# A hybrid encoder layer: narrower edge units in the attention, keys loaded once, the meta tokens' parts side by side, a factor product moved

## The chip, the core and the metric

The kernel runs on one core of a Trainium2 chip. Of the core's engines, TensorE (PE in the profile; its weight loads are listed apart as PEld) does all matrix products and transposes and writes them to PSUM, VectorE (DVE) and ScalarE (ACT) do the elementwise work and bring results out of PSUM, GpSimd (POOL) does small things here, and SyncE (SP) issues nearly all transfers. The metric is the time of one execution in microseconds (us), median of the runs; lower is better.

## The reference

The layer is applied to a prompt of 1024 tokens and a sample of 2048 tokens, each with the same 16 learned meta tokens in front. With `D = 1024`:

```python
xn   = rmsnorm(h, g_pre)
proj = xn @ w_in + b_in                      # 1024 -> 6672 columns
ya   = neighbourhood_attention(q, k, v, rpb) * silu(z)      # 8 heads of 64
yb   = mlstm(qk, v, gates, o) * silu(z)                     # 4 heads of 128, both directions
y    = (sigmoid(ga) * (ya @ w_a) + sigmoid(gb) * (yb @ w_b)) @ w_out
out  = h + rmsnorm(y, g_post)                # meta tokens dropped
```

In the attention the tokens form a grid of 64 columns. A query attends to the 16 meta tokens and to a window of 8 rows by 16 columns around it, with a relative bias. The reference takes query columns in four blocks of 16; each block looks at 32 key columns, which start at column 0, 8, 24 and 32 for the four blocks, and masks those outside a query's own window. For the leftmost block, windows reach from column 0 to 22 (the first 9 queries all have the window 0 to 15); for the rightmost they reach from 40 to 63. So of the 32 key columns of an edge block at most 24 can be in any window.

## The kernel before

All products keep near-float32 precision: each float32 operand is split into a high part (a copy to the type fp32r) and a low part (the difference), and a product is a sum of three: high by high, low by high, high by low. `mm3` (lines 169 to 171) issues such a triple with a weight part stationary and 512 tokens moving; `tm_unit` (lines 590 to 592) issues it with 128 tokens stationary and 256 or 264 weight columns moving.

Two streams are interleaved in program order on TensorE, which is fixed by the program; the other engines' orders come from a scheduler. `dense` yields the projections (`group`, `fm_half`, `tm_unit`) and, later, the output stage (`final`, lines 1569 to 1571 among others). `sparse` yields the mLSTM (`ml`) and the attention (`na`). Each `yield` hands over a cost in us, and `run` lets `dense` go on until it has used up what `sparse` yielded; when `sparse` has ended, the rest of `dense` runs alone. The steps are: mLSTM of the prompt, attention of the prompt, mLSTM of the sample, attention of the sample.

**The attention.** A *head* here is 8 query rows of one attention head (48 of them: 16 for the prompt, 32 for the sample). It takes 11, 12 or 15 key rows plus one row slot for the meta tokens, so 12, 13 or 16 slots. A *unit* is one of the head's four query blocks (192 units). A unit goes through a pipeline, four quarters per unit, `A_NA` = 1.085 yielded after each:

- `na_scores`: two products into one PSUM bank (`sc` or `sm`), with 128 queries stationary and all slots by 32 key columns moving (line 877 with the key's high part doubled in `kd`, line 878 with the low part and the mask rows in `kx`), so 384, 416 or 512 moving columns; then the bias and the row's extreme on VectorE (line 881).
- `na_exp` (ACT, line 891), one unit later `na_scale` (DVE, lines 899 and 900), one more later `na_turn`: four transposes (line 908) into bank `tr`, one for each 8 key columns, and the copy of the high part to `pts` (ACT, 910); `na_low` takes the low part (DVE, 915).
- `na_out`: four products with the values `vt` (line 923) into `sm`; `na_copy` and `na_add` bring the result out (lines 931, 938).

`na_prep` prepares the next head in steps during the units of the current one. The raw keys `kr` arrive in 64 partitions twice (`twice`, line 746: two transfers for the grid's keys, two for the meta tokens' keys), since the score product wants the high part in both halves of `kd`; ACT copies `kd` from `kr` in 128 partitions (line 855) and DVE makes the low part `kx` in 64 (line 857). The meta tokens' keys lie in the row slot at columns 8 to 23 and 32 to 47, so that each block of 32 key columns holds a whole copy, and the mask rows let one copy through.

**The meta tokens** go through `tm_unit` as 16 stationary columns: for each of 8 slices of D three products of 256 or 264 columns (five such units: 40 triples). The result is scaled by the token's factor `rc` and the bias is added in one DVE operation (line 601).

**The opening.** The first group (prompt tokens 0 to 511, then 512 to 1023) is projected before the norm's factors of its tokens are known. The four units of a half write to PSUM, and only when `rwait` has issued the factor product (`rrows`, line 320: ones times a diagonal, which spreads the factors over the partitions) may the results be scaled and leave. Up to then their banks are held: three of tag `pj`, which the next `tm_unit` needs too, and one of `tr`.

Of the kernel before, what the change touches and what calls it, by code (L numbers as in the profile page):

```python
# [42 lines left out]
KC0 = (0, 8, 24, 32)  # L43
OFFC = (15, 7, 7, -1)
# [27 lines left out]
def _consts():  # L72
# [9 lines left out]
    for typ, tl in ((0, 0), (1, 1), (2, R // 8 - 1)):  # L82
# [3 lines left out]
        for si, row in enumerate(slots):  # L86
            for c0 in range(49):
                m = np.full(64, NEG, np.float32)
                if row is None:
                    m[(8 if c0 < 24 else 32):][:NM] = 0.0  # L90
                else:
                    m[c0:c0 + 16] = 0.0
                masks[typ, c0, si] = m
# [27 lines left out]
class K:  # L121
# [231 lines left out]
    def opening(self, xp):  # L353
# [45 lines left out]
        self.wrp = wp, 2  # L399

# [93 lines left out]
    def fm_evac(self, col, s, t0, meta, chunks, ps):  # L494
# [39 lines left out]
        if meta and C_NK <= col < C_NV:  # L534
# [3 lines left out]
            nc.gpsimd.tensor_copy(km[:, 32:48], st[:, :NM])  # L538
# [31 lines left out]
    def tm_unit(self, col, halves, wd):  # L570
# [10 lines left out]
        for j, (x, s, c, n, cnt, tok) in enumerate(todo):  # L581
            st = wp.tile([P, 2, WU], F32, name="stT", bufs=4)
            for a in range(cnt):
                p = self.psum("pj", [P, 512])
                o = p[:n, :wd]
                xs = slice(c + a * P, c + a * P + n)
                for k in range(KT):
                    wh, wl = ws[k // 4][0][:, k % 4, :], ws[k // 4][1][:, k % 4, :]
                    xh, xl = x[0][:, k, xs], x[1][:, k, xs]
                    nc.tensor.matmul(o, xh, wh, start=k == 0, stop=False)  # L590
                    nc.tensor.matmul(o, xh, wl, start=False, stop=False)  # L591
                    nc.tensor.matmul(o, xl, wh, start=False, stop=k == KT - 1)  # L592
# [6 lines left out]
                if s == 0:  # L599
                    r = 8 if tok is None else tok // P + a  # L600
# [5 lines left out]
                yield 12 * C256  # L606

    def tm_store(self, col, wd, s, n, cnt, tok, st):
# [30 lines left out]
        else:  # L639
            if tok is None:  # L640
                for lo in (8, 32):
                    nc.sync.dma_start(self.NVM[lo:lo + NM, f:f + wd], st[:n, 0, :wd])
# [48 lines left out]
    def group(self, s, t0, meta, cols, reuse, nxt):  # L691
# [4 lines left out]
        for j, (kind, c) in enumerate(jobs):  # L696
# [7 lines left out]
            for hf in range(2):  # L704
# [37 lines left out]

    def twice(self, out, d, r0, c0):

        for a in (0, 64):
            self.nc.sync.dma_start(out[a:a + 64], d[r0:r0 + 64, c0:c0 + out.shape[1]])
# [70 lines left out]
    def na_prep(self, np_, s, rows, heads, j):  # L817
# [14 lines left out]
        self.twice(kr[:, rs:rs + nr, :].rearrange("p a b -> p (a b)"), self.NK[s][pr], h0, lo * 64)  # L832
        self.twice(kr[:, ms, :], self.NKM[pr], h0, 0)
# [20 lines left out]
        with self.held():  # L854
            nc.scalar.activation(kd[:, :ns, :], kr[:, :ns, :], AF.Copy)
        yield
        nc.vector.tensor_tensor(kx[0:64, :ns, :], kr[0:64, :ns, :], kd[0:64, :ns, :].bitcast(F32), op=ALU.subtract)
# [9 lines left out]
    def na_scores(self, np_, unit, rows):  # L867
# [8 lines left out]
        so = sc[:, :N].rearrange("p (a b) -> p a b", b=32)  # L876
        nc.tensor.matmul(so, stk[:, cb, :], kd[:, :ns, kc:kc + 32], start=True, stop=False)
        nc.tensor.matmul(so, qb[:, cb, :], self.kx[hh][:, :ns, kc:kc + 32], start=False, stop=True)
# [3 lines left out]
            out=so, in0=so, in1=gt[:, g0:g0 + ns, c0:c0 + 32],  # L882
            op0=ALU.add, op1=ALU.min, scale=-1.0, scalar=3.0e38, accum_out=mx)
        unit[3] = (pr_, mx, N)
        unit[6] = sc

    def na_exp(self, np_, unit):
        nc = self.nc
        (pr_, mx, N), sc = unit[3], unit[6]
        sm = np_.tile([P, 1], F32, name="sm", bufs=4)  # L890
        nc.scalar.activation(pr_[:, :N].rearrange("p (b a c) -> p b a c", b=4, c=8),
                             sc[:, :N].rearrange("p (a b c) -> p b a c", b=4, c=8),
                             AF.Exp, bias=mx, scale=-1.0, accum_out=sm)
        unit[3] = (pr_, sm, N)

    def na_scale(self, np_, unit):
        nc = self.nc
        pr_, sm, N = unit[3]
# [3 lines left out]
    def na_turn(self, np_, unit):  # L902
        nc = self.nc
        pr_, _, N = unit[3]
        ks = N // 4
        pt = self.psum("tr", [P, 4, P])
        for ch in range(4):
            nc.tensor.transpose(pt[:ks, ch, :], pr_[:, ch * ks:(ch + 1) * ks], self.ident)  # L908
        pts = np_.tile([P, 4, 2, P], F32R, name="pts", bufs=2)
        nc.scalar.activation(pts[:ks, :, 0, :], pt[:ks], AF.Copy)  # L910
        unit[4], unit[6] = pts, pt

    def na_low(self, unit):
        pts, pt, ks = unit[4], unit[6], unit[3][2] // 4
        self.nc.vector.tensor_tensor(pts[:ks, :, 1, :], pt[:ks], pts[:ks, :, 0, :].bitcast(F32), op=ALU.subtract)  # L915

    def na_out(self, unit):
        nc = self.nc
        vt, cb, (_, _, N), pts = unit[0][3], unit[2], unit[3], unit[4]
        ks, kc = N // 4, KC0[cb]  # L920
# [858 lines left out]
```

## Time and profile before

| | |
|---|---|
| median of 3 runs | 2786.84 us (2786.1 to 2787.6) |
| profiled execution | 2792.15 us, its span 2790.4 us |
| PE busy | 2764.9 us (99%), 17120 matmuls |
| PEld, DVE, ACT busy | 2461.8 us, 1828.0 us, 1311.8 us |
| attention of the prompt: first to last score product | 758.6 to 1111.1 us, 64 units |
| attention of the sample | 1926.8 to 2656.1 us, 128 units |

In the profile's views a row gives line, engine, operation, output and inputs by the program's names, and sizes. Matmuls overlap: one lasts from its start to the modelled end of its results, while the next has already begun. So what a matmul costs TensorE is read from start to start in the timeline, not from its duration. An "x4" in the timeline is four equal instructions in a row, with the time from the first start to the last end. A window view gives for each stretch its length, then the busy time and count of each engine, the granted clock and the DMA engines' share.

### The profile page before, as it was taken

Reading aid. Unit: us, or ns where it says so; the run is one execution under the profiler, and the core shown is the slowest. Engines: PE = TensorE matmul, PEld = TensorE weight load, DVE = VectorE, ACT = ScalarE, POOL = GpSimd, SP = SyncE. Lnnn points to the kernel's source line nnn. Section 1 sums busy time; section 2 is a strip of 40 time slices with the busy share of each in tenths; the row PEclk is TensorE's granted clock in tenths of the full one; section 3 lists DMA queues with packets and bytes.
Section 4 is the critical chain, followed back from the end, with each engine's and each line's share of the span. In section 5 each row is a group of like instructions: output and inputs, shape, how many; then the busy total and the mean of one; then the engine's idle time right before and its main releaser. Section 6 shows DMA issues by size and latency. Waiting matters only on the chain.

```text
span 2790.4 us, 48772 instructions
## 1 busy us (share of the span) xinstructions
PE 2764.9 (99%) x17120; PEld 2461.8 (88%) x17120; DVE 1828.0 (66%) x5075; ACT 1311.8 (47%) x3183; POOL 16.3 (1%) x103
## 2 busy tenths in 40 slices
PE   9999999999999999999999999999999999999998
PEld 7998898999899988988988888888888988889898
DVE  5232688676556655457767666584679888797954
ACT  5112556445443444255456555463455645445421
POOL 0000000000000000000000000000000000000000
PEclk9999999999999999999999999999999999999999
DMA  9555768755965544685666786666579898988965
GB/s 370 181 186 195 255 199 320 269 179 184 338 216 179 173 151 147 187 300 173 205 199 210 254 290 192 190 197 185 179 228 352 278 324 258 316 276 281 329 236 210
DMA packets 378277, 655.09 MB, mean 235 GB/s; under 512 B 50896, under 2 KB 199840, under 8 KB 378032
## 3 DMA queue, kind: packets, MB, share of 16 engines
q1 hardware_dynamic: 376912, 649.29, 70.5%
q0 software_dynamic: 1120, 2.69, 0.4%
q8 instruction: 135, 2.21, 0.3%
q14 instruction: 110, 0.90, 0.1%
HBM read 449.61 MB, written 202.22 MB: 234 GB/s over the span
## 4 chain that ended last, share of the span: by engine, by line
PE 92%; DMA 5%; DVE 2%; ACT 1%; issue 0%; SPq 0%; DVEq 0%; ACTq 0%
PE pj L169 16%; PE pj L170 16%; PE pj L171 16%; PE pj L590 7%; PE pj L591 7%; PE pj L592 7%; PE sm L923 3%; PE pj L1569 3%; PE pj L1571 3%; PE pj L1570 3%; PE tr L908 3%; DMA wraw<-wu 1%; DMA whi<-wh 1%; PE sm L171 1%; PE sm L170 1%; PE sm L169 1%
## 5 line engine op out<-in xcount | busy, mean ns | idle before, releaser
L169 PE MATMUL pj<-xh,whi 128*128 128x512 f32 (+1 forms) x1792 | 705.4, 394 | 1.5 <-ACT whi L263 1.3
L170 PE MATMUL pj<-xl,whi 128*128 128x512 f32 (+1 forms) x1792 | 689.7, 385 | 0.3 <-DVE xl L335 0.3
L171 PE MATMUL pj<-xh,wlo 128*128 128x512 f32 (+1 forms) x1792 | 688.2, 384 | 0.0
L590 PE MATMUL pj<-whi,xh 128*128 128x256 f32 (+3 forms) x1576 | 449.2, 285 | 1.5 <-ACT st L520 1.5
L591 PE MATMUL pj<-wlo,xh 128*128 128x256 f32 (+3 forms) x1576 | 443.7, 282 | 0.8 <-DMA wlo<-wl 0.8
L592 PE MATMUL pj<-whi,xl 128*128 128x256 f32 (+3 forms) x1576 | 443.6, 282 | 0.0
L171 PEld LDWEIGHTS pj<-xh,wlo 128*128 128x128 f32 x1792 | 337.2, 188 | 71.5 <-DVE wlo L264 0.2
L169 PEld LDWEIGHTS pj<-xh,whi 128*128 128x128 f32 x1792 | 337.3, 188 | 61.8 <-ACT whi L263 2.1
L170 PEld LDWEIGHTS pj<-xl,whi 128*128 128x128 f32 x1792 | 337.7, 188 | 57.5 <-issue 1.0
L590 PEld LDWEIGHTS pj<-whi,xh 128*128 128x128 f32 (+1 forms) x1576 | 293.5, 186 | 3.2 <-ACT st L520 1.9
L591 PEld LDWEIGHTS pj<-wlo,xh 128*128 128x128 f32 (+1 forms) x1576 | 293.1, 186 | 2.1 <-DMA wlo<-wl 1.1
L592 PEld LDWEIGHTS pj<-whi,xl 128*128 128x128 f32 (+1 forms) x1576 | 293.1, 186 | 0.9
L1569 PE MATMUL pj<-whi,mh 128*128 128x256 f32 x768 | 221.6, 289 | 3.6 <-DMA whi<-wh 3.6
L1570 PE MATMUL pj<-wlo,mh 128*128 128x256 f32 x768 | 217.6, 283 | 1.2 <-DMA wlo<-wl 1.2
L1571 PE MATMUL pj<-whi,mlo 128*128 128x256 f32 x768 | 217.7, 283 | 0.0
L915 DVE TENSOR_TENSOR pts<-tr,pts 96x512 fp32r<-96x512 f32 (+2 forms) x192 | 131.8, 686 | 96.0 <-ACT pts L910 95.1
L910 ACT ACTIVATE pts<-tr 96x512 fp32r<-96x512 f32 (+2 forms) x192 | 113.9, 593 | 136.8 <-PE tr L908 136.5
L169 PE MATMUL pj<-yh,whi 128*128 128x512 f32 x384 | 154.4, 402 | 0.0
L1569 PEld LDWEIGHTS pj<-whi,mh 128*128 128x128 f32 x768 | 146.4, 191 | 6.2 <-DMA whi<-wh 4.7
L171 PE MATMUL pj<-yh,wlo 128*128 128x512 f32 x384 | 151.4, 394 | 0.0
L170 PE MATMUL pj<-yl,whi 128*128 128x512 f32 x384 | 150.9, 393 | 0.0
L1570 PEld LDWEIGHTS pj<-wlo,mh 128*128 128x128 f32 x768 | 146.7, 191 | 3.0 <-DMA wlo<-wl 1.4
(283 smaller groups left out, 4990.4 us busy)
## 6 DMA issues: line engine op xcount, KB each, us to landing
whi<-wh SPq DMA_DIRECT2D x176, 512.0 KB
wlo<-wl SPq DMA_DIRECT2D x176, 512.0 KB
wraw<-wu SPq DMA_DIRECT2D x64, 512.0 KB
wh<-whi SPq DMA_DIRECT2D x64, 512.0 KB
wl<-wlo SPq DMA_DIRECT2D x64, 512.0 KB
gt<-st SPq DMA_DIRECT2D x96, 256.0 KB
tg<-gt SPq DMA_DIRECT2D x96, 256.0 KB
xt<-xt SPq DMA_DIRECT2D x32, 512.0 KB
```

Of the source, the lines that this page charges most:

```text
L169: mm(out, ah, bh, start=start, stop=False)
L170: mm(out, ah, bl, start=False, stop=False)
L171: mm(out, al, bh, start=False, stop=stop)
L590: nc.tensor.matmul(o, xh, wh, start=k == 0, stop=False)
L591: nc.tensor.matmul(o, xh, wl, start=False, stop=False)
L592: nc.tensor.matmul(o, xl, wh, start=False, stop=k == KT - 1)
L908: nc.tensor.transpose(pt[:ks, ch, :], pr_[:, ch * ks:(ch + 1) * ks], self.ident)
L910: nc.scalar.activation(pts[:ks, :, 0, :], pt[:ks], AF.Copy)
L915: self.nc.vector.tensor_tensor(pts[:ks, :, 1, :], pt[:ks], pts[:ks, :, 0, :].bitcast(F32), op=ALU.subtract)
L1569: nc.tensor.matmul(o, mh[:, k, xs], wh, start=k == 0, stop=False)
L1570: nc.tensor.matmul(o, mh[:, k, xs], wl, start=False, stop=False)
L1571: nc.tensor.matmul(o, ml[:, k, xs], wh, start=False, stop=k == KT - 1)
```

## The change

- **Edge units.** The first and the fourth block of a head take 24 key columns, from column 0 and 40 on (`NKB` holds the number of 8-column pieces, 3 or 4). Scores, bias, exponent and scale work on 24 columns per slot, with three transposes and three value products. The second copy of the meta tokens' keys moves to columns 40 to 55, the value rows and their zero rows accordingly.
- **Keys loaded once.** `kr` is loaded in one half (two transfers in place of four); ACT makes the high part in 64 partitions and copies it to the other 64 in a second operation.
- **Meta parts side by side.** A small tile `xmp` holds the meta tokens' high part in columns 0 to 15, zeros, and the low part in columns 32 to 47 of 48 stationary columns. Two products (by the weight's high and low part) replace three; the two partial results, in different partitions, are added by an ACT copy and a DVE addition ahead of the scaling. The new low-by-low term is part of the result for those partitions. `xmp` is filled in the opening and given back when the attention begins.
- **Factor product a unit sooner.** For the second half of the first group, `rwait` is called after the last step of unit 2 in place of the third step of unit 3, and the three units' results leave then; unit 3 alone goes to `tr`.

```diff
-KC0 = (0, 8, 24, 32)
-OFFC = (15, 7, 7, -1)
+KC0 = (0, 8, 24, 40)
+NKB = (3, 4, 4, 3)
+OFFC = (15, 7, 7, 7)
...
@@ opening
+        nc.gpsimd.memset(self.xmp[:, :, NM:2 * NM].bitcast(F32), 0.0)
+        for a in range(2):
+            nc.vector.tensor_copy(self.xmp[:, :, 2 * NM * a:2 * NM * a + NM], x[a][:, :, :NM].bitcast(F32))
...
@@ tm_unit
+                    if tok is None:
+                        both = self.xmp[:, k]
+                        nc.tensor.matmul(o, both, wh, start=k == 0, stop=False)
+                        nc.tensor.matmul(o, both, wl, start=False, stop=k == KT - 1)
...
-                        yield 12 * C256
+                        yield (8 if tok is None else 12) * C256
...
+                if tok is None:
+                    nc.scalar.activation(st[:n, 1, :wd], p[2 * NM:2 * NM + n, :wd], AF.Copy)
+                    nc.vector.tensor_tensor(st[:n, 1, :wd], p[:n, :wd], st[:n, 1, :wd], op=ALU.add)
+                    nc.vector.scalar_tensor_tensor(st[:n, 0, :wd], st[:n, 1, :wd], self.rc[:n, 8:9], bb[:n, :wd], op0=ALU.mult, op1=ALU.add)
...
@@ group
-                    lu = 3 if hf else 2
...
-                        if late is not None and u == lu and q == 2:
+                        if late is not None and u == 2 and q == 2 + hf:
                             self.rwait[todo[hf][:2]]()
-                    if late is not None and u == lu:
+                    if late is not None and u == 2:
                         for evac in late:
                             evac()
-                        late = tags = None
+                        late = None
+                        tags = iter(("tr",)) if hf else None
...
@@ na_prep
-        self.twice(kr[:, rs:rs + nr, :].rearrange("p a b -> p (a b)"), self.NK[s][pr], h0, lo * 64)
-        self.twice(kr[:, ms, :], self.NKM[pr], h0, 0)
+        nc.sync.dma_start(kr[0:64, rs:rs + nr, :].rearrange("p a b -> p (a b)"), self.NK[s][pr][h0:h0 + 64, lo * 64:(lo + nr) * 64])
+        nc.sync.dma_start(kr[0:64, ms, :], self.NKM[pr][h0:h0 + 64, :])
...
-            nc.scalar.activation(kd[:, :ns, :], kr[:, :ns, :], AF.Copy)
+            nc.scalar.activation(kd[0:64, :ns, :], kr[0:64, :ns, :], AF.Copy)
         yield
+        nc.scalar.activation(kd[64:128, :ns, :], kd[0:64, :ns, :].bitcast(F32), AF.Copy)
...
@@ na_scores
-        N, kc, g0 = ns * 32, KC0[cb], (5, 1, 0)[typ]
+        kc, nb, g0 = KC0[cb], NKB[cb], (5, 1, 0)[typ]
+        w, N = 8 * nb, 8 * nb * ns
...
@@ na_turn
-        for ch in range(4):
+        for ch in range(nb):
             nc.tensor.transpose(pt[:ks, ch, :], pr_[:, ch * ks:(ch + 1) * ks], self.ident)
...
@@ na_out
-        for ch in range(4):
+        for ch in range(nb):
             nc.tensor.matmul(av[:, :256], vt[:ks, kc // 8 + ch].rearrange("p a b -> p (a b)"),
```

Three places in the instruction orders show what moves. On TensorE in the opening, before, the factor product (`ones`, into `sm`) stands six matmuls ahead of the end of the second half's fourth unit (the one that writes `tr`); line 590 is the next `tm_unit`:

```order
L171 MATMUL tr<-xh,wlo 128x512
L320 MATMUL sm<-xr,ones 128x512
L169 MATMUL tr<-xh,whi 128x512
L170 MATMUL tr<-xl,whi 128x512
L171 MATMUL tr<-xh,wlo 128x512
L169 MATMUL tr<-xh,whi 128x512
L170 MATMUL tr<-xl,whi 128x512
L171 MATMUL tr<-xh,wlo 128x512
L590 MATMUL pj<-whi,xh 128x264
```

and now it stands right behind the third unit, ahead of all 24 of the fourth (lines 170 to 172 are the former 169 to 171):

```order
L170 MATMUL pj<-xh,whi 128x512
L171 MATMUL pj<-xl,whi 128x512
L172 MATMUL pj<-xh,wlo 128x512
L321 MATMUL sm<-xr,ones 128x512
L170 MATMUL tr<-xh,whi 128x512
L171 MATMUL tr<-xl,whi 128x512
```

It has moved past 18 matmuls; nothing else of the opening has changed its place on this engine. On TensorE in the attention of the sample, before, in the first head, a unit's four transposes and the four value products of the unit ahead of it stand so:

```order
L908 MATMUL tr<-ident,prb 96x128 x4
L923 MATMUL sm<-pts,vt 128x256 x4
L169 MATMUL pj<-xh,whi 128x512
L170 MATMUL pj<-xl,whi 128x512
L171 MATMUL pj<-xh,wlo 128x512
```

and now, in the same head, for edge units:

```order
L919 MATMUL tr<-ident,prb 96x128 x3
L170 MATMUL pj<-xh,whi 128x512
L171 MATMUL pj<-xl,whi 128x512
L172 MATMUL pj<-xh,wlo 128x512
L170 MATMUL pj<-xh,whi 128x512
L171 MATMUL pj<-xl,whi 128x512
L172 MATMUL pj<-xh,wlo 128x512
L934 MATMUL sm<-pts,vt 128x256 x3
```

There are three of each, and six matmuls of the projection now stand between them where none stood: the two streams mesh at another phase, since the meta units yield less. Over the whole program TensorE's list loses 40 meta products, 96 transposes and 96 value products, and of 384 score products 192 are narrower. On ScalarE in the sample's attention beside the output stage, before, a head's key copy (`kd<-kr`) stands between the transposes' copies (`pts`), the output stage's (`mh`), and `yg`:

```order
L910 ACTIVATE pts<-tr 128x4x128
L855 ACTIVATE kd<-kr 128x1024
L1537 ACTIVATE mh<-tg 128x512
L931 ACTIVATE yg<-sm 64x8x16
L910 ACTIVATE pts<-tr 128x4x128
```

and now:

```order
L921 ACTIVATE pts<-tr 128x3x128
L863 ACTIVATE kd<-kr 64x1024
L865 ACTIVATE kd<-kd 64x1024
L942 ACTIVATE yg<-sm 64x8x16
L870 ACTIVATE vt<-vr 128x8x64
```

The copy is two operations of 64 partitions in a row, ahead of `yg` and of the values' copy.

More of the change, by code (lines that the diff above doesn't have):

```diff
@@ L89, in _consts @@
                 if row is None:
-                    m[(8 if c0 < 24 else 32):][:NM] = 0.0
+                    m[(8 if c0 < 24 else 40):][:NM] = 0.0
                 else:
@@ L588, in tm_unit @@
                     wh, wl = ws[k // 4][0][:, k % 4, :], ws[k // 4][1][:, k % 4, :]
[L589 to L592, printed above, removed]
+                    if tok is None:
+                        both = self.xmp[:, k]
+                        nc.tensor.matmul(o, both, wh, start=k == 0, stop=False)
+                        nc.tensor.matmul(o, both, wl, start=False, stop=k == KT - 1)
+                    else:
+                        xh, xl = x[0][:, k, xs], x[1][:, k, xs]
+                        nc.tensor.matmul(o, xh, wh, start=k == 0, stop=False)
+                        nc.tensor.matmul(o, xh, wl, start=False, stop=False)
+                        nc.tensor.matmul(o, xl, wh, start=False, stop=k == KT - 1)
                     if k == 3:
@@ L881, in na_scores @@
         nc.vector.tensor_tensor_reduce(
-            out=so, in0=so, in1=gt[:, g0:g0 + ns, c0:c0 + 32],
+            out=so, in0=so, in1=gt[:, g0:g0 + ns, c0:c0 + w],
             op0=ALU.add, op1=ALU.min, scale=-1.0, scalar=3.0e38, accum_out=mx)
-        unit[3] = (pr_, mx, N)
+        unit[3] = (pr_, mx, nb, 8 * ns)
         unit[6] = sc
```

54 lines of the change are left out of this document (28 added, 26 removed).

## The prediction

> **What bounds the kernel now.** I read the page's busy times and its chain of waits first, then the windows by stage, then the timeline for what a matmul costs.
>
> ```profile
> PE 2764.9 (99%) x17120; PEld 2461.8 (88%) x17120; DVE 1828.0 (66%) x5075; ACT 1311.8 (47%) x3183; POOL 16.3 (1%) x103
> ...
> PE 92%; DMA 5%; DVE 2%; ACT 1%; issue 0%; SPq 0%; DVEq 0%; ACTq 0%
> ...
> 1300.00:2020.00 720.00, 720.00 (x3765) 609.74 (x3764) 480.97 (x1544) 380.50 (x978) 3.59 (x18) 1.00 0.65 209
> 2020.00:2300.00 280.00, 275.05 (x1634) 241.39 (x1633) 233.91 (x527) 153.69 (x342) 1.02 (x2) 0.99 0.89 294
> 2300.00:2560.00 260.00, 255.11 (x1697) 232.57 (x1696) 213.88 (x513) 132.34 (x333) 1.02 (x2) 0.99 0.93 287
> ```
>
> TensorE is the bound: busy for 99% of the span and 92% of the chain that ended last. So an instruction taken from TensorE's list shortens the run by its slot, if nothing else takes the slot up. The windows say where that is least sure. From 1300 to 2020 us TensorE never pauses. From 2020 to 2560 us, where the sample's attention runs beside the output stage, VectorE is busy for 234 of 280 us (84%), the DMA engines for 0.89 to 0.93 of the time, and TensorE is idle for 5.0 us (280 − 275.05) and 4.9 us (260 − 255.11).
>
> **What a slot is worth.** Matmuls overlap, so starts count. These are score products of 512 and of 384 columns in the timeline:
>
> ```profile
> 2146.13 0.40 PE L877 MATMUL sm<-kd,stk 128*128 128x512 f32 x1
> 2146.36 0.40 PE L878 MATMUL sm<-kx,qB 128*128 128x512 f32 x1
> 2146.60 0.39 PE L169 MATMUL pj<-yh,whi 128*128 128x512 f32 x1
> ...
> 2080.07 0.34 PE L877 MATMUL sc<-kd,stk 128*128 128x384 f32 x1
> 2080.25 0.34 PE L878 MATMUL sc<-kx,qB 128*128 128x384 f32 x1
> 2080.43 0.39 PE L169 MATMUL pj<-xh,whi 128*128 128x512 f32 x1
> ```
>
> 512 columns take (2146.60 − 2146.13)/2 = 0.235 us, 384 take (2080.43 − 2080.07)/2 = 0.18, so a column is worth 0.055/128 = 0.43 ns. No row has the new widths 288 and 312; I extend this line down to them. For the transposes and the value products the timeline merges four; the groups by form give one's own duration:
>
> ```profile
> 1001.76 0.60 PE L908 MATMUL tr<-ident,prb 128*104 128x128 f32 x4
> 2083.64 0.64 PE L923 MATMUL sm<-pts,vt 96*128 96x256 f32 x4
> ...
> L908 PE MATMUL tr<-ident,prb 128*104 128x128 f32 x256 | 38.3, 272 | 0.0
> L923 PE MATMUL sm<-pts,vt 96*128 96x256 f32 x256 | 42.8, 289 | 0.0
> ```
>
> Three starts lie between the first and the last of four: a transpose's slot is (0.60 − 0.272)/3 = 0.109 us, a value product's (0.64 − 0.289)/3 = 0.117. The meta tokens' products:
>
> ```profile
> 97.32 0.28 PE L590 MATMUL pj<-whi,xh 128*16 128x264 f32 x1
> 97.44 0.28 PE L591 MATMUL pj<-wlo,xh 128*16 128x264 f32 x1
> 97.56 0.28 PE L592 MATMUL pj<-whi,xl 128*16 128x264 f32 x1
> ```
>
> 0.12 us each with 16 stationary columns. The rows above with 128 stationary columns and 256 moving have 0.117, so 48 stationary columns won't cost more.
>
> **Edge units.** 96 of the 192 units are edge units, 32 for each of the three head sizes. Transposes: 96 × 0.109 = 10.5 us. Value products: 96 × 0.117 = 11.2 us. Scores: two products lose 128, 104 or 96 columns in 32 units each, 64 × (128 + 104 + 96) = 20992 columns × 0.43 ns = 9.0 us. That is 30.7 us, 0.32 per edge unit.
>
> The Trainium skill, page "TensorE: Matmul & The Clock Gate", section "Back-to-back issue gap", speaks against this: it puts a sustained stream of weight load and matmul at about 81 ns for 128 columns and 131 ns for 512, an eighth of a nanosecond a column. By it (98 ns at 256, on its line) transposes would give 7.8 us, value products 9.4, scores 2.7 and the meta products 3.9, an estimated 23.8 us in place of the 35.5 below. The trace disagrees with its slots, 0.235 us at 512 columns; the rows decide.
>
> On VectorE and ScalarE these units shrink as well. The bias operation, for instance, goes from 512 to 384 columns:
>
> ```profile
> L881 DVE CUSTOM_DVE_ANT_1 sc<-sc,gt 128x512 f32<-128x512 f32 x32 | 22.2, 692 | 5.2 <-PE sc L878 4.8
> L881 DVE CUSTOM_DVE_ANT_1 sc<-sc,gt 128x384 f32<-128x384 f32 x32 | 18.1, 565 | 21.3 <-PE sc L878 15.7 <-DMA gt<-rpb 4.3 <-issue 0.6
> ```
>
> That is 0.13 us less for the widest units, and the scale and the low part (line 915) shrink as far, so VectorE does not become tighter relative to TensorE. I take nothing extra for it, since neither engine sets the end.
>
> **Meta parts.** 40 products × 0.12 = 4.8 us. The result's way out grows by an ACT copy and a DVE addition of 256 columns, five times; of that width the groups by form have
>
> ```profile
> L603 DVE TENSOR_TENSOR stT<-pj,bb 128x256 f32<-128x256 f32 x96 | 40.5, 422 | 37.6 <-PE pj L592 35.8
> L1599 ACT ACTIVATE sqj<-pj 128x256 bf16<-128x256 f32 x96 | 36.5, 380 | 86.9 <-PE pj L1571 86.3
> ```
>
> so 0.8 us each time. The bank is one of three of tag `pj`; two more `tm_unit` groups of 24 products (24 × 0.12 = 2.9 us each) run before it is wanted, which hides it. Uncovered it would cost 5 × 0.8 = 4 us. The two fills of `xmp` come on VectorE ahead of line 335, which waits anyway (second row of the next fence: 1.99 us idle for the tokens' transfer); each is about as long as the subtraction ahead of it on the same 128 columns (first row, 0.29). Cost zero; without the gap 0.6 us.
>
> ```profile
> 4.49 0.29 DVE L380 TENSOR_TENSOR xl<-xm,xh 128x128 fp32r<-128x128 f32 x1 [0.38 <-ACT xh L379]
> 6.77 1.41 DVE L335 SCALAR_TENSOR_TENSOR xl<-xt,gpre,xh 128x512 fp32r<-128x512 f32 x2 [1.99 <-ACT xh L334]
> ```
>
> **Factor product.** In the timeline of the opening:
>
> ```profile
> 55.49 1.02 PE L320 MATMUL sm<-xr,ones 128*128 128x512 f32 x2
> 56.55 0.60 ACT L321 ACTIVATE rr<-sm 128x512 f32<-128x512 f32 x1 [4.17 <-PE sm L320]
> 57.18 1.90 DVE L508 TENSOR_TENSOR pj<-pj,rr 128x512 f32<-128x512 f32 x3 [3.52 <-ACT rr L321]
> 57.51 0.40 PE L171 MATMUL tr<-xh,wlo 128*128 128x512 f32 x1
> 58.70 1.83 ACT L520 ACTIVATE st<-pj,bfm 128x512 f32<-128x512 f32 x3
> 59.42 0.39 PE L590 MATMUL pj<-whi,xh 128*128 128x264 f32 x1 [1.51 <-ACT st L520]
> ```
>
> Line 590 wants a `pj` bank. Without the wait it would start 0.23 us behind 57.51, at 57.74, so 1.68 us are lost. Moved up by 18 matmuls of 0.23, or 4.2 us, the product starts at 51.3 and the banks begin to leave at about 54.5, before 57.7: the whole 1.68 us goes. Late next is nothing that I see.
>
> **Keys loaded once.** Per head, two DMA issues less on SP's queue: those queued behind them (values, bias, weights) start earlier; and 240 KB plus the meta tokens' keys less to move. Against it a second ACT operation of the same columns, which I take to last as long in 64 partitions as the old one in 128: 1.06 us in the widest heads. What waits behind it on ACT is `yg` and the values' copy `vt`, and TensorE's next head waits for `kd`:
>
> ```profile
> L855 ACT ACTIVATE kd<-kr x48: 829/891/1067, 753.7 to 2631.6; 128x768 fp32r<-128x768 f32 x16, 128x832 fp32r<-128x832 f32 x16, 128x1024 fp32r<-128x1024 f32 x16
> ...
> 2072.05 0.83 ACT L855 ACTIVATE kd<-kr 128x768 fp32r<-128x768 f32 x1
> ...
> 777.42 0.83 ACT L855 ACTIVATE kd<-kr 128x768 fp32r<-128x768 f32 x1
> 778.31 0.45 PE L877 MATMUL sc<-kd,stk 128*128 128x384 f32 x1
> 778.38 0.94 DVE L857 TENSOR_TENSOR kx<-kr,kd 64x768 fp32r<-64x768 f32 x1
> 779.37 0.44 PE L878 MATMUL sc<-kx,qB 128*128 128x384 f32 x1 [0.62 <-DVE kx L857]
> ```
>
> The head copied at 2072.05 has `kd` at 2072.88 and its first score product at 2080.07 (above): 7.2 us of slack, which hides 0.9. The second head, at 778, has 0.06; but there line 878 waits for `kx` until 779.37 anyway, and the second copy would end at 779.1. So nothing is added on the path. From below, the lighter transfers could save part of the waits for transfers (the 2.75 us of the next fence); from above, the mean of 829, 891 and 1056 to 1067 ns, 0.93 us, in each of 48 heads: 44.5 us. I take zero, by the 7.2 us.
>
> **Sum.** 30.7 + 4.8 + 1.7 = 37.2 us. The profiled execution took 2792.15 us (span 2790.4, 1.75 around it), so by it 2755.0; the median of the runs, 5.3 us lower, gives 2786.84 − 37.2 = **2749.6 us**, which I forecast. What stays open are TensorE's stalls in the late stage. These are the longest, as the timeline brackets them:
>
> ```profile
> 2087.70 0.49 PE L877 MATMUL sm<-kd,stk 128*128 128x384 f32 x1 [2.04 <-DVE yg L938]
> 2152.14 0.74 PE L923 MATMUL sm<-pts,vt 128*128 128x256 f32 x4 [2.15 <-ACT prb L891]
> 2428.98 0.39 PE L1569 MATMUL pj<-whi,mh 128*128 128x256 f32 x1 [2.75 <-DMA whi<-wh]
> ```
>
> Each has another cause: VectorE's queue, ScalarE's, a weight transfer. The change re-meshes the two streams (the place in the orders where six matmuls now stand between transposes and value products), so these come anew at other places; I expect as many, give or take 5 us.
>
> **Rivals.**
>
> *The late stage is paced by others.* If transfers and VectorE set the pace from 2020 to 2560 us, slots freed there turn into waits. At 730 us (1926.8 to 2656.1) for 128 units a unit takes 5.7 us; 540/5.7 = 95 units, 47 of them edge units, × 0.32 = 15 us lost: 2764.6. For it: the DMA share of 0.93. Against it: TensorE still works 98% there, and keys and edge units relieve both others.
>
> *Narrower products keep their slot.* If the score products take as long with 288 columns as with 384, only whole products count: 37.2 − 9.0 gives 2758.6. Against it: 0.18 beside 0.235. This is the direction of the Trainium skill's rule above, by which the time would be 2786.84 − 23.8 − 1.7 = 2761.3 as an estimate.
>
> *The late stalls go.* Fewer transfers and less VectorE work could take away the 9.9 us of idle time in the two windows: 2739.7.
>
> *Slower: the second key copy is waited for.* If at each head ScalarE finishes `kd` too late by the copy, 44.5 us come in and 37.2 go: 2794.1. It decides where less than 0.93 us lies between the copy and the first score product, and it outweighs the gain from 40 heads of 48 on (37.2/0.93). For it: the 0.06 us at 778. Against it: the 7.2 us at 2080.
>
> *The freed slots don't shorten the run at all*, since something per unit paces the attention: 2786.8. TensorE's 720.00 of 720 us speaks against it.
>
> **How the numbers follow.** The forecast 0.69 (its own range 2744 to 2756), late stage 0.15, slots kept 0.05, stalls gone 0.07, slower 0.03, nothing 0.01. A measurement tells about 0.2%, 5.6 us, from no change. All but the last two cases are faster by more: 0.96; same 0.01; slower 0.03. The range goes from the stalls' end, 2739, to just past the late stage's 2764.6, at 2765; it holds the forecast, the kept slots, most of the late stage's case and half of the stalls'.
>
> **What would show it.** After: 232 matmuls fewer (40 + 96 + 96); score products of 288 columns from start to start in 0.14 us (0.18 − 96 × 0.43 ns); three transposes in 0.49 and three value products in 0.52 as merged rows; meta pairs at 0.12; no wait ahead of the first `tm_unit` product; first score products of a head microseconds behind the second `kd` copy; TensorE busy about 2728 us. Wrong would be: idle time in 2020 to 2560 us well over 10 us, or score products that wait for `kd`.

## The result and the profile after

The changed kernel takes **2749.48 us** (median of 4 runs, 2747.49 to 2751.54), the kernel before 2786.47 us on the same chip (4 runs, 2784.52 to 2787.6): a ratio of 0.9868, 95% interval 0.9851 to 0.9885, so 37 us less. Forecast: 2749.6 us, 37.2 us less. The total is right; the experiments below show that two of its terms were not, with opposite signs.

The page of the changed kernel, its busy times, the shares of the chain that ended last, and what the transfers moved:

```profile
PE 2727.7 (99%) x16888; PEld 2431.3 (88%) x16888; DVE 1801.1 (65%) x5082; ACT 1342.9 (49%) x3236; POOL 16.9 (1%) x104
...
PE 94%; DMA 3%; DVE 2%; ACT 1%; issue 0%; SPq 0%; DVEq 0%; ACTq 0%
...
DMA packets 370595, 644.30 MB, mean 234 GB/s; under 512 B 46288, under 2 KB 195232, under 8 KB 370352
```

TensorE has 232 matmuls fewer (17120 − 16888) and is busy 37.2 us less (2764.9 − 2727.7). It is still the bound: 99% of the span, and its share of the chain went up from 92% to 94% while the transfers' fell from 5% to 3%.

The windows of the changed kernel (length, then busy time and count of PE, PEld, DVE, ACT and POOL, the granted clock, the DMA share, GB/s):

```profile
1300.00:2020.00 720.00, 719.18 (x3759) 608.24 (x3758) 475.48 (x1520) 385.12 (x981) 3.61 (x18) 1.00 0.65 209
2020.00:2300.00 280.00, 278.29 (x1752) 248.73 (x1751) 239.08 (x559) 173.62 (x387) 1.02 (x2) 1.00 0.90 299
2300.00:2560.00 260.00, 255.24 (x1654) 232.05 (x1653) 214.89 (x542) 142.68 (x347) 1.02 (x2) 0.99 0.87 280
```

In the late stage TensorE idles 1.7 and 4.8 us where it idled 5.0 and 4.9 before. VectorE is a little busier in the first of these windows than before (239 of 280 us, before 234), with more of its operations in the same time (559 against 527). It did not become the bound.

The timeline of the changed kernel, at the places that the prediction named:

```profile
56.95 0.39 PE L172 MATMUL tr<-xh,wlo 128*128 128x512 f32 x1
57.19 0.28 PE L599 MATMUL pj<-whi,xh 128*128 128x264 f32 x1
...
768.37 0.29 PE L887 MATMUL sm<-kd,stk 128*128 128x288 f32 x1
768.50 0.29 PE L888 MATMUL sm<-kx,qB 128*128 128x288 f32 x1
768.63 0.39 PE L170 MATMUL pj<-xh,whi 128*128 128x512 f32 x1
...
2390.24 0.49 PE L919 MATMUL tr<-ident,prb 128*128 128x128 f32 x3
2390.49 0.60 PE L934 MATMUL sm<-pts,vt 128*128 128x256 f32 x3
```

The first `tm_unit` product (now line 599) follows the triple ahead of it by 0.24 us: the wait of 1.51 us is gone. A score product of 288 columns takes (768.63 − 768.37)/2 = 0.13 us from start to start. Transposes and value products come in threes, the transposes in 0.49 us. Three value products take 0.52 us, or 0.60 where transposes stand right ahead of them (in the kernel before, four take 0.64 and 0.72).

**A count by starts.** To compare kernels I worked out two sums from each trace: every matmul taken at the median distance to the next start that its form has over all traces together, a form being its tiles and sizes (*slots*), and what is left of the distances from start to start (*stalls*: idle time, and matmuls that ran slower than their form does). Stalls are also given for three stages. Each row is one profiled execution; that of before lies at 2792.15 us, in the upper part of the runs seen of it (2783 to 2795), so differences from it of a few microseconds in stalls are not firm. A second execution of the changed kernel has 32.3 us of stalls where the row has 34.4, and 4.9 where it has 6.4 from 740 to 1120 us. "Old count" is explained with the meta parts below.

| us | slots | stalls | to 65 | 740 to 1120 | 1900 to 2640 |
|---|---|---|---|---|---|
| before | 2742.0 | 38.2 | 4.2 | 2.9 | 17.5 |
| after | 2705.8 | 34.4 | 1.9 | 6.4 | 12.1 |
| edge units alone | 2710.4 | 32.3 | 4.1 | 2.3 | 12.1 |
| scores alone narrow | 2732.2 | 29.3 | 4.0 | 2.1 | 9.8 |
| meta parts alone | 2737.4 | 37.8 | 3.9 | 7.7 | 11.1 |
| meta parts, old count | 2737.4 | 35.5 | 3.9 | 2.6 | 15.4 |
| factor product alone | 2742.0 | 35.1 | 2.5 | 2.5 | 16.3 |
| keys alone | 2742.0 | 30.1 | 3.9 | 2.8 | 9.9 |
| keys alone, idle loads | 2742.0 | 35.8 | 3.7 | 2.9 | 15.7 |
| after, middle blocks 24 too | 2674.3 | 36.4 | 2.2 | 7.1 | 12.4 |
| after, second copy four times | 2705.8 | 65.4 | 2.8 | 10.8 | 34.1 |
| after, old count | 2705.8 | 28.1 | 2.4 | 1.8 | 10.5 |

### The profile page after: what moved, and what is told of

It reads as the page before. It is cut to its first block, busy times and chain, and to the rows that moved or that the text cites. A ratio compares the mean times of both kernels' runs of the same rounds, so it can differ in the third digit from the quotient of the medians.

```text
span 2749.8 us, 48160 instructions
## 1 busy us (share of the span) xinstructions
PE 2727.7 (99%) x16888; PEld 2431.3 (88%) x16888; DVE 1801.1 (65%) x5082; ACT 1342.9 (49%) x3236; POOL 16.9 (1%) x104
## 3 DMA queue, kind: packets, MB, share of 16 engines
q0 software_dynamic: 1120, 2.69, 0.4%
## 4 chain that ended last, share of the span: by engine, by line
PE 94%; DMA 3%; DVE 2%; ACT 1%; issue 0%; SPq 0%; DVEq 0%; ACTq 0%
PE pj L170 17%; PE pj L171 17%; PE pj L172 17%; PE pj L599 7%; PE pj L600 7%; PE pj L601 7%; PE pj L1581 3%; PE pj L1582 3%; PE pj L1580 3%; PE sm L934 3%; PE tr L919 2%; DMA wlo<-wl 1%; PE sm L172 1%; PE sm L171 1%; PE sm L170 1%; PE sm L1368 1%
## 5 line engine op out<-in xcount | busy, mean ns | idle before, releaser
L599 PE MATMUL pj<-whi,xh 128*128 128x256 f32 (+1 forms) x1536 | 439.7, 286 | 0.9 <-DMA whi<-wh 0.9
L600 PE MATMUL pj<-wlo,xh 128*128 128x256 f32 (+1 forms) x1536 | 433.2, 282 | 1.5 <-DMA wlo<-wl 1.5
L601 PE MATMUL pj<-whi,xl 128*128 128x256 f32 (+1 forms) x1536 | 433.0, 282 | 0.0
L600 PEld LDWEIGHTS pj<-wlo,xh 128*128 128x128 f32 x1536 | 290.0, 189 | 2.2 <-DMA wlo<-wl 2.0
L599 PEld LDWEIGHTS pj<-whi,xh 128*128 128x128 f32 x1536 | 290.0, 189 | 1.7 <-DMA whi<-wh 1.1
L601 PEld LDWEIGHTS pj<-whi,xl 128*128 128x128 f32 x1536 | 289.8, 189 | 0.0
L926 DVE TENSOR_TENSOR pts<-tr,pts 96x384 fp32r<-96x384 f32 (+2 forms) x192 | 119.0, 620 | 77.5 <-ACT pts L921 75.3
L921 ACT ACTIVATE pts<-tr 96x384 fp32r<-96x384 f32 (+2 forms) x192 | 103.8, 541 | 123.0 <-PE tr L919 122.4
```

The source lines that it names most:

```text
L921: nc.scalar.activation(pts[:ks, :nb, 0, :], pt[:ks, :nb], AF.Copy)
L926: self.nc.vector.tensor_tensor(pts[:ks, :nb, 1, :], pt[:ks, :nb], pts[:ks, :nb, 0, :].bitcast(F32), op=ALU.subtract)
```

## The experiments

Times are medians. Every ratio is against the kernel before on the same chip. "Less" and "more" in us are differences of medians against it, unless said otherwise.

### The four parts, each alone

The edge units alone (all of that part of the diff, `NKB` and what follows from it):

```diff
-KC0 = (0, 8, 24, 32)
+KC0 = (0, 8, 24, 40)
+NKB = (3, 4, 4, 3)
```

> The kernel before with the edge units alone narrowed to 24 key columns (keys still loaded twice, meta parts and factor product as before). My theory: each of TensorE's slots that goes shortens the run, 10.5 us of transposes, 11.2 of value products, 9.0 of score columns: 30.7 us less than before. Rival, late stage paced by VectorE and the transfers: 15 us of this is lost, so 15 to 16 us less. Rival, narrower products keep their slot: 21.7 us less.

Measured: 2758.18 us, ratio 0.9895 (0.988 to 0.991), 30.2 us less. The slots fell by 2742.0 − 2710.4 = 31.6 us; the sum in the prediction was 30.7.

The keys loaded once, alone (the two transfers in place of four are those of the change and are left out here):

```diff
-            nc.scalar.activation(kd[:, :ns, :], kr[:, :ns, :], AF.Copy)
+            nc.scalar.activation(kd[0:64, :ns, :], kr[0:64, :ns, :], AF.Copy)
...
+        nc.scalar.activation(kd[64:128, :ns, :], kd[0:64, :ns, :].bitcast(F32), AF.Copy)
```

> The kernel before with the keys loaded once and copied by ScalarE to the other half, nothing else. My theory: no change (within 3 us), since the first score product of a head comes 7 us behind its keys; first score products don't wait except in the first head or two. Rival, the second copy is waited for at each head: up to 44.5 us slower. Second rival, the lighter transfers shorten waits for weights: 2 to 5 us faster.

Measured: 2781.02 us, ratio 0.9974 (0.9966 to 0.9983), 7.3 us less. The forecast of nothing (within 3 us) falls; the rival of 2 to 5 us has the right sign, and only the lower end of the interval (4.7 to 9.5 us) reaches into it. The slots are the same, so all of it is in the stalls, and by the table nearly all of these lie in the late stage.

The meta parts side by side, alone:

```diff
+                        both = self.xmp[:, k]
+                        nc.tensor.matmul(o, both, wh, start=k == 0, stop=False)
+                        nc.tensor.matmul(o, both, wl, start=False, stop=k == KT - 1)
...
-                        yield 12 * C256
+                        yield (8 if tok is None else 12) * C256
```

> The kernel before with the meta tokens' parts side by side, nothing else. My theory: 40 products of 0.12 us fewer, 4.8 us less than before, and 48 stationary columns at the same 0.12 us as 16. Rival, the longer way out of PSUM holds a bank that the next group wants: the gain shrinks by up to 4 us, to about 1 us, and the group behind a meta unit shows a wait.

Measured: 2787.24 us, ratio 0.9998 (0.9989 to 1.0007), 1.1 us less, which is no change that can be told. The slots did fall by 4.6 us, but the stalls from 740 to 1120 us rose from 2.9 to 7.7: the gain was made and given back where the prompt's attention starts.

The factor product a unit sooner, alone:

```diff
-                        if late is not None and u == lu and q == 2:
+                        if late is not None and u == 2 and q == 2 + hf:
```

> The kernel before with the factor product a unit sooner, nothing else. My theory: the one wait of 1.68 us ahead of the first product with 128 stationary tokens goes, 1.7 us less than before, which the times alone hardly tell from no change; the trace shows that product start 0.23 us behind the one before it. Rival: the wait moves, to the fourth unit's bank or to a later product, and shows there with about the same length.

Measured: 2786.87 us, ratio 0.9998 (0.9989 to 1.0007), 1.5 us less; by itself it can't be told from nothing. In the count by starts the opening's stalls fell from 4.2 to 2.5 us, the expected 1.7.

The four ratios multiplied give 0.9895 × 0.9974 × 0.9998 × 0.9998 = 0.9865, the ratio of the whole is 0.9868. So the parts add up as far as the intervals tell (some 5 us either way for the whole).

### What an edge unit is worth, and whether the late stage takes it

All four blocks at 24 columns (this leaves out the last 8 key columns of each middle block, so the attention is computed with fewer keys there):

```diff
-NKB = (3, 4, 4, 3)
+NKB = (3, 3, 3, 3)
```

> The changed kernel with the two middle units of each head narrowed to 24 key columns as well; the last 8 key columns of each middle block are left out of the attention. 96 more units lose one transpose, one value product and 24 or more score columns a slot. My theory: the same price again, 0.32 us a unit, 30.7 us less than the changed kernel (about 2718.5). Rival, VectorE and transfers pace the late stage by now: at most 16 us less, with TensorE's idle time between 2020 and 2560 us clearly over 20 us.

Measured: 2720.13 us, ratio 0.9748 (0.9733 to 0.9762). Against the changed kernel's ratios of 0.9868 here and 0.9855 in its second run below, that is 30 to 34 us less again. The slots fell by 31.5 us. The late stage of this kernel:

```profile
2020.00:2300.00 280.00, 277.37 (x1753) 249.13 (x1752) 241.47 (x592) 174.66 (x401) 1.02 (x2) 1.00 0.94 311
2300.00:2560.00 260.00, 255.15 (x1636) 231.12 (x1635) 215.90 (x553) 140.16 (x351) 1.02 (x2) 0.99 0.92 298
```

It is idle for 7.5 us (2.6 and 4.9) where the changed kernel has 6.5, far from the 20 us of the rival, though the transfers' share went up to 0.94 and 0.92. The late stage still gives TensorE's time back; the rival in which VectorE or the transfers pace it is refuted for this size of change too.

Only the scores narrow: bias, exponent and scale work on 24 columns, but four transposes and four value products stay, the fourth repeating the third (so the attention's result counts the last piece twice):

```diff
         for ch in range(4):
-            nc.tensor.transpose(pt[:ks, ch, :], pr_[:, ch * ks:(ch + 1) * ks], self.ident)
+            c = min(ch, nb - 1)
+            nc.tensor.transpose(pt[:ks, ch, :], pr_[:, c * ks:(c + 1) * ks], self.ident)
```

> The kernel before with narrow edge units in scores, bias, exponent and scale alone: still four transposes and four value products, of which the fourth repeats the third piece, so the edge blocks' results are left wrong by that piece. It prices the columns by themselves. My theory: 20992 columns at 0.43 ns, 9.0 us less than before. Rival, a narrower product keeps its slot: no change. By the rule of the Trainium skill, page TensorE: Matmul & The Clock Gate, section Back-to-back issue gap, an estimate of 2.7 us.

Measured: 2775.08 us, ratio 0.9948 (0.9934 to 0.9963): 14.5 us less by the ratio, 10.3 to 18.4 by its interval, which is more than any of the three expected. The time alone can't price the columns, since the stalls fell too. The slots can: 2742.0 − 2732.2 = 9.8 us, near the 9.0. So nothing (the slot kept) and the page's 2.7 us both fall. The rest is late stalls, 9.8 us against 17.5 in the trace of before and 12.1 with all of the edge part. Of the 7.7 us against before some 3.7 are stretches in which TensorE ran at half rate behind a wait (three in that trace, one in this; the last section has more on them). Why this kernel fares better is not settled.

### The keys: two questions

Why did they give anything? First the changed kernel without this part:

```diff
-        nc.sync.dma_start(kr[0:64, ms, :], self.NKM[pr][h0:h0 + 64, :])
+        self.twice(kr[:, ms, :], self.NKM[pr], h0, 0)
...
+            nc.scalar.activation(kd[:, :ns, :], kr[:, :ns, :], AF.Copy)
```

> The changed kernel with the keys part undone: loaded in both halves by four transfers, one ScalarE copy in 128 partitions. My theory: the same as the changed kernel within 3 us (37 us below the kernel before); the first head's score product no longer waits for the second copy, 1 us. Rival, the second copy costs at many heads: faster than the changed kernel by more than 5 us. Rival, the lighter transfers helped: slower by 2 to 5 us.

Measured: 2758.71 us, ratio 0.9883 (0.9866 to 0.99). Beside the changed kernel's 0.9868 and 0.9855 the keys are worth 4 to 8 us there as well, where no more than 3 us was expected, though the intervals overlap. The trace has 37.4 us of stalls, against 34.4 and 32.3 in the two of the changed kernel.

Then the keys alone, but with the two dropped transfers issued again into the half of `kr` that nobody reads:

```diff
         nc.sync.dma_start(kr[0:64, ms, :], self.NKM[pr][h0:h0 + 64, :])
+        nc.sync.dma_start(kr[64:128, ms, :], self.NKM[pr][h0:h0 + 64, :])
```

(and the same for the grid's keys).

> The keys loaded once alone, but the two transfers that it dropped are issued again, into the lower half of kr, where nobody reads them; kd still comes from the two ScalarE copies. Bytes and SP's issues are those of the kernel before. Theory (the 7 us that the keys gave come from two issues less on SP's queue and from fewer bytes, through shorter waits for transfers in the late stage): the time goes back to the kernel before, ratio 0.999 to 1.001. Rival (they come from the order of ScalarE's and VectorE's work, which the second copy changes): still some 7 us faster, ratio 0.997 to 0.998.

Measured: 2788.83 us, ratio 1.0001 (0.9992 to 1.001). The whole gain is gone, with ScalarE's two copies still in place. By the traces TensorE's order is the same in these two kernels, and ScalarE's differs at 31 of 3231 places. So the 7 us are the transfers', not the second copy's effect on the order. Whether it is the bytes or SP's issues was not tried apart.

Where they act is seen in TensorE's waits between 1900 and 2640 us (line waited for: us in total, times, longest). With the keys alone:

```profile
PE pj L1565 <- DMA whi<-wh: 3.0, 2, 1.5
PE sm L919 <- ACT prb L887: 2.3, 2, 1.6
PE sm L873 <- DVE yg L934: 1.9, 1, 1.9
```

With the idle loads:

```profile
PE pj L1567 <- DMA whi<-wh: 5.3, 1, 5.3
PE sm L921 <- ACT prb L889: 2.3, 2, 1.6
PE sm L875 <- DVE yg L936: 1.9, 1, 1.9
```

Only the wait for the output stage's weights differs: 3.0 us in two pieces of 1.5, against 5.3 in one. That is 2.3 us. The stalls differ by more, 9.9 against 15.7, because of TensorE's rate behind the waits. Windows of 10 us around that weight wait, TensorE alone (length, busy time, granted clock, DMA share, GB/s), for the keys alone:

```profile
2415.00:2425.00 10.00, 7.66 (x61) 1.00 1.04 336
2425.00:2435.00 10.00, 9.31 (x75) 1.00 0.76 204
```

with the idle loads:

```profile
2425.00:2435.00 10.00, 7.81 (x46) 0.66 1.04 308
```

and for the kernel before:

```profile
2425.00:2435.00 10.00, 6.92 (x42) 0.83 1.03 329
```

After the waits of 1.5 us the granted clock stays at 1.00. After 5.3 us (and after the 2.75 us of before) it is 0.66 and 0.83 in the window. By the distances from start to start the matmuls behind the 5.3 us lose another 2.0 us. So a long wait can be paid twice: in its length and in the rate behind it. Together that is 4.3 of the 5.8 us.

The other 1.5 us lie behind a wait that is the same in both traces, the one for VectorE, 1.87 and 1.88 us, which ends at 2087 us. From 2087 to 2097 us the granted clock is 1.00 with the keys alone and 0.83 with the idle loads. That this comes from the transfers too is not shown.

The second question is the copy's price, the rival that ended on the slower side. The second copy four times over:

```diff
-        nc.scalar.activation(kd[64:128, :ns, :], kd[0:64, :ns, :].bitcast(F32), AF.Copy)
+        for _ in range(4):
+            nc.scalar.activation(kd[64:128, :ns, :], kd[0:64, :ns, :].bitcast(F32), AF.Copy)
```

> The changed kernel with ScalarE's second key copy made four times over (the same data), 3 x 0.93 = 2.8 us more of ScalarE per head. My theory: the slack between the last copy and a head's first score product (3.3 us or more in 47 of 48 heads) hides most of it; the first head pays 2.5 us; in all 0 to 15 us slower than the changed kernel. Rival, the copy stands on the path at each head: 48 x 2.8 = 134 us slower.

Measured: 2781.86 us, ratio 0.9965 (0.9953 to 0.9978), 27 to 31 us above the changed kernel's two runs by the ratios. That is more than the 0 to 15 us expected, and far from the 134 of a copy that is waited for at each head. Who waited for the copy, in the changed kernel (first the copies: count, shortest, median and longest in ns, first and last start; then us and times):

```profile
L865 ACT ACTIVATE kd<-kd x48: 842/898/1071, 753.5 to 2596.1; 64x768 fp32r<-64x768 f32 x16, 64x832 fp32r<-64x832 f32 x16, 64x1024 fp32r<-64x1024 f32 x16
...
  PE sc L887: 0.9, 1
```

and with four copies:

```profile
L866 ACT ACTIVATE kd<-kd x192: 830/898/1065, 758.9 to 2631.2; 64x768 fp32r<-64x768 f32 x64, 64x832 fp32r<-64x832 f32 x64, 64x1024 fp32r<-64x1024 f32 x64
...
  PE sc L888: 28.5, 19
```

One copy makes TensorE wait at one head of 48; 2.8 us more of them per head make it wait at 19 heads, for 28.5 us, which is about the loss. So the cover is real, but at 19 heads it is less than those 2.8 us: the mechanism of the slower rival exists, and it decides the time once the copy is a few microseconds longer.

### The meta parts: what gave the gain back

The planner is `run`, which interleaves the two streams by the costs that they yield. The meta parts alone, with the count that a half unit yields to it put back to 12 widths of 256 columns, here and where a unit's other half yields:

```diff
-                yield (8 if tok is None else 12) * C256
+                yield 12 * C256
```

> The meta parts side by side alone, with one thing put back: a half of a meta unit still counts as 12 widths of 256 columns to the planner that deals the sample's pieces out between the prompt's, not 8, though it now issues 8 matmuls. The product rows are the same 40 fewer as with the meta parts alone, so the slots give 40 x 0.12 = 4.8 us again. Theory (the gain of the meta parts was given back because the smaller count shifts the pieces against each other, so that the prompt's attention starts before its keys and weights are there: waits of 2.2 and 1.2 us ahead of lines 598 and 599 at 775 to 777 us): about 4 us faster than before, ratio 0.998 to 0.9990, and no waits of over 1 us for whi or wlo between 740 and 800 us. Rival (the way out by ScalarE and VectorE, or anything else in the 40 products' own place): no faster than the meta parts alone, ratio 0.9995 to 1.0005, and the waits from 740 to 800 us as there.

Measured: 2782.39 us, ratio 0.9977 (0.9968 to 0.9986), 6.5 us less; the interval is clear of that with the new count (0.9989 to 1.0007). So it is the count. TensorE's waits between 740 and 1120 us, with the new count:

```profile
PE pj L598 <- DMA whi<-wh: 2.0, 1, 2.0
PE pj L599 <- DMA wlo<-wl: 0.7, 1, 0.7
PE sc L890 <- DVE kx L869: 0.5, 1, 0.5
```

with the old one:

```profile
PE sc L890 <- DVE kx L869: 0.6, 1, 0.6
PE pj L599 <- DMA wlo<-wl: 0.4, 1, 0.4
```

The two kernels issue the same instructions in another order, and with the smaller count the start of the prompt's attention meets weights that have not landed (why just these come late was not followed further). The expectation of about 4 us lies at the lower end of the interval, 3.9 to 8.9 us.

The changed kernel again, on the same chip as the next one:

> The changed kernel itself once more, on the same chip as the other three, so that the next one can be compared with it: ratio 0.985 to 0.988, some 37 us faster than before.

Measured: 2748.3 us (2746.08 to 2749.45), ratio 0.9855 (0.9841 to 0.9868), 40.6 us less.

The changed kernel with the old count:

> The changed kernel with the planner's old count of 12 widths for a half of a meta unit, everything else as changed. Theory (the smaller count is what costs the meta parts their gain): 3 to 4 us less than the changed kernel on the same chip, with the stalls from 740 to 1120 us, 6.4 us by the distances from start to start in the changed kernel, back to about 3. Rival (the stalls at the start of the prompt's attention come from elsewhere, or others take their place): the same as the changed kernel within 1 us.

Measured: 2746.04 us (2744.47 to 2747.08), ratio 0.9847 (0.9834 to 0.9861): 2.3 us below the changed kernel, between the 3 to 4 us of the theory and the 1 us of the rival. The intervals of the two ratios overlap, so the time alone doesn't settle that it is the better version. The traces agree with the theory. The waits from 740 to 1120 us in the changed kernel:

```profile
PE pj L600 <- DMA wlo<-wl: 1.5, 2, 0.9
PE sc L887 <- ACT kd L865: 0.9, 1, 0.9
PE pj L599 <- DMA whi<-wh: 0.9, 1, 0.9
```

and with the old count:

```profile
PE sc L887 <- ACT kd L865: 0.9, 1, 0.9
```

The weight waits are gone, and the stalls there fall from 6.4 us (4.9 in the second execution) to 1.8. It is the fastest kernel measured here that computes the whole reference.

## Why the prediction was right, and where it was not

**The bound.** Right. TensorE's instructions carried the change: 36.2 us of slots went (2742.0 − 2705.8), against 30.7 + 4.8 = 35.5 in the sum.

**Edge units, 30.7 us.** Right: 30.2 alone, 31.6 in slots. The line through 512 and 384 columns, extended down to 288, gave 0.14 us; it is 0.13. The page "TensorE: Matmul & The Clock Gate" of the Trainium skill, section "Back-to-back issue gap", led to 23.8 us for edge units and meta parts together; the slots gave 36.2, and those of the narrow scores 9.8 where it had 2.7, so the rows were the better guide.

**Meta parts, 4.8 us.** The slots were right (4.6; with 48 stationary columns a product of 264 still takes 0.12 us), and the result's way out cost nothing that can be seen. What failed is the cost list: it had the 40 products, the way out and the fill of `xmp`, but not the count that a half unit hands to the planner, which the same lines of the diff change from 12 to 8. With that count the parts alone gave 1.1 us instead of 4.8; with the old count 6.5 were measured. It is an edit that issues nothing and still changes when weights are wanted.

**Factor product, 1.7 us.** Right in its place: the wait of 1.51 us is gone and the opening's stalls fell by 1.7 alone and 2.3 in the whole change. Its effect on the time is below what the runs resolve.

**Keys loaded once, 0 us.** Wrong: 7.3 us less. The cover for the second copy was read rightly: it held at 47 of 48 heads. The head that had none was the first, not the second, where I had looked:

```profile
753.51 0.84 ACT L865 ACTIVATE kd<-kd 64x768 fp32r<-64x768 f32 x1
...
754.40 0.40 PE L887 MATMUL sc<-kd,stk 128*128 128x288 f32 x1 [0.89 <-ACT kd L865]
```

That costs 0.9 us once. The step that failed is the gain from the lighter transfers: it was put at zero, with part of the 2.75 us wait as its most, so a wait was priced at its length. With the transfers back, the 7.3 us were gone. In the traces one wait of 5.3 us for weights (2.75 in the kernel before) became two of 1.5, and the half-rate stretch behind the long one is missing. That is 4.3 of the 5.8 us by which the late stalls of the two kernels differ; where the rest comes from stays open.

**The sum.** 37.2 forecast, 37 measured (by the ratio's interval 32 to 42), by an offset: 7.3 us too little for the keys and 3.7 too much for the meta parts. With both put right the sum is 40.8; the second run of the changed kernel gave 40.6 less. So that the first came out within 1 us of the forecast is luck, and the range was right since the errors were small beside the slots.

**The late stage.** "As many stalls, give or take 5 us": by starts 17.5 before, 12.1 after, just past that, with the reserve that the profiled execution of before lies high among its runs. The rival that had the late stage paced by VectorE or the transfers is refuted by the two kernels with fewer slots (30.2 us for the edge units alone, 30 to 34 more with narrow middle blocks), the rival of narrower products keeping their slot by the slots of the scores alone, the rival of a copy waited for at every head by the one wait above. The rival of late stalls that go was half true: idle time from 2020 to 2560 us fell from 9.9 to 6.5 us, not to nothing.

**What would have shown it.** The 232 matmuls, 0.13 to 0.14 us, the merged threes (0.60 in place of 0.52 us where transposes stand right ahead), the missing wait and TensorE's 2728 us all came. The row that spoke against a step was there too: one score product waited for `kd`.

## What to carry to other kernels

Cost a wait by its length and by the clock behind it: here a wait of 5.3 us for weights cost another 2 us in the matmuls that followed, so a saved transfer can be worth more than the wait that it shortens. List what an edit tells the planner beside what it issues; a count in a yield moved 5 us of stalls without an instruction. A total that comes out right says little about its terms, so run each part alone before the next prediction leans on one.

## What the runs showed of the hardware

**A wait of about 2 us can halve TensorE's rate for some microseconds.** The changed kernel, behind its longest wait in the late stage:

```profile
2393.49 0.38 PE L1580 MATMUL pj<-whi,mh 128*128 128x256 f32 x1 [2.41 <-DMA whi<-wh]
...
2399.46 0.41 PE L1580 MATMUL pj<-whi,mh 128*128 128x256 f32 x1
2399.67 0.41 PE L1581 MATMUL pj<-wlo,mh 128*128 128x256 f32 x1
...
2401.06 0.28 PE L1582 MATMUL pj<-whi,mlo 128*128 128x256 f32 x1
2401.18 0.28 PE L1580 MATMUL pj<-whi,mh 128*128 128x256 f32 x1
```

Products of 256 columns run 0.21 us apart (2399.46 to 2399.67) and then 0.12 again (2401.06 to 2401.18); the granted clock from 2396 to 2399 us is 0.50. Over such a stretch mostly 1.6 to 2.7 us are lost beyond the wait, by the distances from start to start. The length of the wait alone does not decide. Two waits of 2.04 us end at 2087.70 us in the kernel before and at 2085.88 with the factor product alone; the windows of 10 us from there, first before, then the other:

```profile
2087.00:2097.00 10.00, 9.29 (x39) 0.83 0.99 324
```

```profile
2085.00:2095.00 10.00, 9.12 (x47) 1.00 1.03 328
```

The same wait, once with a granted clock of 0.83 behind it and once with 1.00; the pair of 1.87 and 1.88 us above is another. Waits up to 1.6 us mostly passed without it. It may be one source of the scatter between executions of one kernel. The Trainium skill, page "TensorE: Matmul & The Clock Gate", section "Part 1: The HAM clock gate (the "warmup" mystery)", puts the drop to half rate behind an idle window of about 3.4 us that runs freely and does not start anew with a kernel. The free window would agree with the same wait ending both ways; on the length the traces differ, with drops behind 1.88, 2.04, 2.41 and 2.75 us.

**ScalarE's slack at the heads is thin in this kernel.** 2.8 us more of copies per head cost 28.5 us of waits at 19 heads, though ScalarE is busy for only 49% of the span of the changed kernel.
